# Mixing the first gate pair's products with the spatial gate's in a one-layer decoder kernel

## The chip, the cores and the metric

The kernel runs on one core of one Trainium2 chip. The metric is device time in microseconds (us), the median of three runs. Five engines work from queues of their own, each in the order in which its instructions were written: TensorE (PE in the profile, its weight loads PEld), VectorE (DVE), ScalarE (ACT), GpSimd (POOL) and SyncE (SP), which here only issues transfers (DMA).

## The reference

One layer over a sequence of 1024 positions and 1024 features, all in float32:

```
h = rmsnorm(x)
[q | k | v | u | s | gate_a | gate_b] = h @ w_in
A = sliding-window attention(q, k, v)            (window 128, 8 heads, ALiBi, sinks)
B = gelu(u) * (tril(W_s) @ rmsnorm(gelu(s)) + b) (per channel group, in chunks of 128 positions)
x = x + (sigmoid(gate_a) * (A @ w_oa) + sigmoid(gate_b) * (B @ w_ob)) @ w_out
x = x + down( silu(conv_g) * conv_v ),  conv = causal depthwise width-3 conv of up(rmsnorm(x))
```

The change lies between B, the spatial gate, and the projections gate_a and gate_b.

## The kernel before

Every matrix product is made in three TensorE passes: each float32 operand is split into a high part (rounded to the type that TensorE multiplies at full rate) and a low part (what is left), and high·high, high·low and low·high are added. A split is an ACT copy that makes the high part (`copy_hi`, L76) and a subtraction on DVE or POOL that makes the low part.

The gate projections, 16 output tiles of 128 features by 1024 positions, are computed in eight pairs: a pair takes one tile of gate_b and the same tile of gate_a. Each pair is a two-by-two block product by Winograd's form of Strassen's scheme: seven products instead of eight. A product (`Blocks.prod`, L916) is 12 matmuls of 128x512: four blocks of the inner dimension, three passes each. The left operands are weights: A11 and A12 are the tile of gate_b, A22 is half of the tile of gate_a, and S1 to S4 are sums of them, made on POOL. The right operands are B11, B21, B22 (parts of the input, split long before) and T1 to T4 (sums of parts of the input, made in place in the tiles `xa`). The seven products are A11·B11, A12·B21, S4·B22, A22·T4, S1·T1, S2·T2 and S3·T3. `split_p` makes the high and low parts of A11 and A12, `split_q` those of S1 and A22, `split_r` those of S2 and S4 (tile `gax`), `split_s3` those of S3; their low parts come from POOL (L885). `x_split` (L747) makes those of T1 to T4 in two halves of 128x1024 each, with both low parts on DVE (L756).

The spatial gate works in four channel tiles t and two halves of the sequence, so eight products (t, half). `sgu_seed` (L812, an ACT copy) fills a PSUM tile with the bias b, `sgu_mm` (L818) adds 12 matmuls of 128x256 onto it, and `sgu_mul` (L827, two DVE instructions) multiplies the result into `uT`. A seed can be written when the PSUM tile that it takes has been read by the `sgu_mul` that used it last. The right factors are the v rows: eight row blocks s, each passed through gelu (`v_gelu`), normed (`v_norm`) and split (`v_split`) into `vsh` and `vsl`.

The order is written out by hand, and nothing reorders it. `v_phase` (L767) computes the v rows, with the products (0,0), (1,0) and (2,0) between them, and other preparation hung on its steps by the table `X_WORK` (the first half of T1 at step 5). Then come (3,0) and (0,1) to (3,1) one after another (L1709 to L1714), the second half of T1 and both of T3, and then `gates` (L1104): `first_gate_pair` (L993) and seven times `gate_pair` (L1028). In `first_gate_pair` T2 and T4 are split on DVE while the products run. A pair prepares the weights of the next (`nx`). T1, T2 and T4 each take a tile of the pool whose tiles carry the tag Y, and T4 can be written only when one of the raw tiles `xa` has been read for the last time. PSUM holds four tiles of 128x1024: two in pool psA and, once the v rows are through, two in pool psC.

Of the kernel before, what the change touches and what calls it, by code (L numbers as in the profile page):

```python
# [10 lines left out]
F = mybir.dt.float32  # L11
# [30 lines left out]
def body(ctx, tc, nc, a):  # L42
# [33 lines left out]
    def copy_hi(dst, src, scale=1.0):  # L76
        return nc.scalar.activation(dst, src, AF.Copy, scale=scale)  # L77

    def mm3(out, wh, wl, mh, ml, first, last, **kw):

        nc.tensor.matmul(out, wh, mh, start=first, stop=False, **kw)  # L81
        nc.tensor.matmul(out, wh, ml, start=False, stop=False, **kw)  # L82
        nc.tensor.matmul(out, wl, mh, start=False, stop=last, **kw)  # L83
# [655 lines left out]

    def v_norm(s):  # L740
        nc.vector.scalar_tensor_tensor(vg_[s], vg_[s], vss_[s][:, 0:1], sg_b, op0=ALU.mult, op1=ALU.mult)

    def v_split(s):
        copy_hi(vsh[:, s, :], vg_[s])
        nc.vector.tensor_tensor(vsl[:, s, :], vg_[s], vsh[:, s, :].bitcast(F), op=ALU.subtract)

    def x_split(n, ks=range(2)):  # L747
        r, c = {"T1": (0, L), "T3": (0, H), "T2": (1, H), "T4": (1, L)}[n]
        if n not in xb:
            xb[n] = zr[0].tile([128, 2, 4, 512], R, tag="Z", name="T3") if n == "T3" else \  # L750
                Y(n, R, [128, 2, 4, 512])
        for k in ks:
            kk = slice(2 * k, 2 * k + 2)
            src = xr_raw[r][:, kk, c]
            copy_hi(xb[n][:, 0, kk, :], src)
            nc.vector.tensor_tensor(xb[n][:, 1, kk, :], src, xb[n][:, 0, kk, :].bitcast(F), op=ALU.subtract)  # L756
# [55 lines left out]
    def sgu_seed(t, half):  # L812

        pm = pms[t, half] = PS("pm")
        nc.scalar.activation(pm.rearrange("p (n i) -> p n i", i=128),
                             bs_b[:, t:t + 1, :].to_broadcast([128, 8, 128]), AF.Copy)
# [23 lines left out]
    class Left:  # L840
# [152 lines left out]
    def first_gate_pair():  # L993

        w, nx = g_left[0], g_left[1]
        q = Blocks(w.w, xb)
        e = PS("pe")
        psum["P"].insert(0, psum["P"].pop())
        m5, m7 = e[:, L], e[:, H]
# [14 lines left out]
        nx.split_p()
        q.prod(m7, "S3", "T3")
        nc.scalar.copy(x7, m5)
        nc.vector.tensor_tensor(q.g1, x7, q.g1, op=ALU.add)
        nc.vector.tensor_tensor(x7, x7, m7, op=ALU.add)
# [682 lines left out]
    jobs.append((None, 0, None))  # L1701
    with tc.manual_schedule():
        v_phase()
        psB.__exit__(None, None, None)
        psum["C"] = tc.tile_pool(name="psC", bufs=2, space=bass.MemoryType.PSUM, reuse_waits="tile")
        psC = psum["C"].__enter__()
        psum["P"] = [psC, psC, psA, psA]
        psum["H"] = None
        order = [(3, 0)] + [(t, 1) for t in range(4)]  # L1709
        for i, m in enumerate(order):  # L1710
            if i < 4:
                sgu_seed(*order[i + 1])
            sgu_mm(*m)
            sgu_mul(*m)  # L1714
        x_split("T1", (1,))
        x_split("T3")
        sg_cm.__exit__(None, None, None)
        gates_open()
        psum["P"] = [psC, psC, psA, psA]
        g_left[1].load_p()  # L1720
# [70 lines left out]
```

## Time and profile before

| what | value |
|---|---|
| median of 3 runs | 1215.3 us (1214.7 to 1215.97) |
| the profiled execution, its own time | 1215.15 us |
| its span, first to last instruction | 1213.4 us |
| granted TensorE clock, mean over the span | 0.994 |
| TensorE busy | 1188.4 us, 98% of the span |
| DVE, POOL, ACT busy | 894.8, 568.6, 542.4 us |

A row of the timeline gives the start in us from the span's beginning, the duration in us, the engine, the line of the kernel, the operation, the output and the inputs by tile name, and the shapes; `xN` says that N equal instructions stand merged, and brackets hold the idle time of the engine ahead of the instruction and what ended it. `pm` is a PSUM tile of the spatial gate, `pz` and `pe` are PSUM tiles of the gate pairs, `T` is a tile of T1 to T4 (and of other right operands), `x` of the L920 rows is the input's split tiles, `ph`, `pl`, `qh`, `ql`, `s3h`, `s3l` are weight parts, `lp`, `lq`, `lr` raw weights. A row of waits gives who waited, for whom, the us in total, how often, and the longest. A row of windows gives for a stretch the busy us and the instructions of each engine, the granted clock (1.00 is full), the share of DMA and its rate.

### The profile page before, as it was taken

To read this page: it belongs to the slowest core of one execution; us is meant where nothing else is said; L and a number is where in the kernel's file an instruction comes from. 1 tells how busy PE (TensorE), PEld (TensorE's weight loads), DVE (VectorE), ACT (ScalarE), POOL (GpSimd) and SP (SyncE) were. 2 spreads that over 40 slices of the span, in tenths; PEclk is the share of its full clock that TensorE was granted. 3 is DMA by queue.
4 is the path that set the end of the run, shared out by engine and by line. 5 is a ranking of instruction groups with operands and counts; after the bars stand their busy time and mean duration, and the time that the engine had idled before them with its cause. 6 is when DMAs were issued, how large, how long until landed. Compare 5 with 4: busy or idle time off the path is not lost.

```text
span 1213.4 us, 15834 instructions
## 1 busy us (share of the span) xinstructions
PE 1188.4 (98%) x5866; PEld 1005.1 (83%) x5866; DVE 894.8 (74%) x1033; ACT 542.4 (45%) x830; POOL 568.6 (47%) x360
## 2 busy tenths in 40 slices
PE   9999999889999999999999999999999999999998
PEld 8889989868887888888788888888888888888886
DVE  7688966764465665568787888877888888776674
ACT  8455575733444312223544444444544445524331
POOL 2467583277766522334765756657565642000000
PEclk9999999989999999999999999999999999999999
DMA  7010143125777897442223324233342358975472
GB/s 280 21 53 19 53 140 122 54 77 173 251 256 270 295 343 274 159 161 104 88 97 112 137 102 144 95 114 125 110 147 87 122 173 276 383 252 191 143 227 73
DMA packets 78989, 191.27 MB, mean 158 GB/s; under 512 B 8896, under 2 KB 9152, under 8 KB 78912
## 3 DMA queue, kind: packets, MB, share of 16 engines
q1 hardware_dynamic: 78912, 190.26, 45.0%
q8 instruction: 46, 0.75, 0.3%
q14 instruction: 31, 0.25, 0.1%
HBM read 139.63 MB, written 50.59 MB: 157 GB/s over the span
## 4 chain that ended last, share of the span: by engine, by line
PE 84%; DVE 7%; ACT 2%; DMA 1%; issue 1%; POOL 0%; SPq 0%; DVEq 0%; ACTq 0%
PE pz L920 42%; PE pd L1601 10%; PE pdy L1601 7%; PE px L81 2%; PE po L82 2%; PE po L81 2%; PE px L83 2%; PE px L82 2%; PE po L83 2%; DMA ls<-wup 1%; PE pvs L81 1%; DVE T L756 1%; PE pvs L83 1%; PE pvs L82 1%; PE pq L81 1%
## 5 line engine op out<-in xcount | busy, mean ns | idle before, releaser
L920 PE MATMUL pz<-T,qh 128*128 128x512 f32 x464 | 142.8, 389 | 0.0
L885 POOL TENSOR_TENSOR pl<-lp,ph 128x1024 fp32r<-128x1024 f32 x30 | 73.6, 2452 | 83.6 <-ACT ph L77 83.5
L920 PE MATMUL pz<-B,ph 128*128 128x512 f32 x352 | 109.5, 392 | 0.0
L920 PEld LDWEIGHTS pz<-T,qh 128*128 128x128 f32 x464 | 87.1, 188 | 18.0
L920 PE MATMUL pz<-T,ql 128*128 128x512 f32 x232 | 90.2, 389 | 0.0
L98 POOL TENSOR_TENSOR wjl<-wj,wjh 128x512 fp32r<-128x512 f32 (+1 forms) x24 | 40.6, 1692 | 95.7 <-ACT wjh L77 95.7
L885 POOL TENSOR_TENSOR ql<-lq,qh 128x1024 fp32r<-128x1024 f32 x30 | 77.6, 2587 | 14.5 <-ACT qh L77 14.5
L920 PEld LDWEIGHTS pz<-B,ph 128*128 128x128 f32 x352 | 65.3, 188 | 15.4 <-ACT x L1449 1.9
L935 DVE TENSOR_TENSOR pz<-pz,rstd_b 128x1024 f32<-128x1024 f32 x60 | 73.9, 1232 | 4.6 <-ACT rstd_b L131 2.5
L885 POOL TENSOR_TENSOR s3l<-s,s3h 128x512 fp32r<-128x512 f32 x30 | 41.2, 1373 | 71.9 <-ACT s3h L77 64.0
L920 PE MATMUL pz<-T,s3h 128*128 128x512 f32 x232 | 71.4, 389 | 0.0
L920 PE MATMUL pz<-B,pl 128*128 128x512 f32 x176 | 68.5, 389 | 0.0
L1601 PE MATMUL pd<-bh,ah 128*128 128x512 f32 x176 | 68.5, 389 | 0.0
L1601 PE MATMUL pd<-bl,ah 128*128 128x512 f32 x176 | 68.5, 389 | 0.0
L1601 PE MATMUL pd<-bh,al 128*128 128x512 f32 x176 | 68.5, 389 | 0.0
L920 PE MATMUL pz<-T,AX 128*128 128x512 f32 x264 | 64.9, 396 | 0.0
L920 PE MATMUL pz<-B,AX 128*128 128x512 f32 x264 | 63.4, 389 | 0.0
L77 ACT ACTIVATE qh<-lq 128x1024 fp32r<-128x1024 f32 x30 | 31.9, 1062 | 64.8 <-issue 35.1
L920 PEld LDWEIGHTS pz<-T,AX 128*128 128x128 f32 x264 | 50.6, 192 | 10.6
L920 PEld LDWEIGHTS pz<-B,AX 128*128 128x128 f32 x264 | 49.5, 188 | 10.3
L1307 DVE SCALAR_TENSOR_TENSOR tv<-pz,cp,tv 128x1023 f32<-128x1023 f32 (+1 forms) x44 | 56.2, 1278 | 0.8
L1307 DVE SCALAR_TENSOR_TENSOR tg<-pz,cp,tg 128x1023 f32<-128x1023 f32 (+1 forms) x44 | 56.2, 1278 | 0.8
(334 smaller groups left out, 3563.7 us busy)
## 6 DMA issues: line engine op xcount, KB each, us to landing
ls<-wup SPq DMA_DIRECT2D x22, 512.0 KB, 5.4
sum<-ls SPq DMA_DIRECT2D x22, 512.0 KB, 4.9
lp<-wup SPq DMA_DIRECT2D x22, 512.0 KB, 3.5
ra<-wdown SPq DMA_DIRECT2D x44, 256.0 KB, 4.7
b<-T SPq DMA_DIRECT2D x44, 256.0 KB, 3.7
B<-tv SPq DMA_DIRECT2D x33, 256.0 KB, 2.0
T<-tt SPq DMA_DIRECT2D x33, 256.0 KB, 2.1
b<-B SPq DMA_DIRECT2D x33, 256.0 KB, 3.2
```

Source lines behind the costliest of these rows:

```text
L77: return nc.scalar.activation(dst, src, AF.Copy, scale=scale)
L81: nc.tensor.matmul(out, wh, mh, start=first, stop=False, **kw)
L82: nc.tensor.matmul(out, wh, ml, start=False, stop=False, **kw)
L83: nc.tensor.matmul(out, wl, mh, start=False, stop=last, **kw)
L98: nc.gpsimd.tensor_tensor(l[:, :nk, :], r[:, :nk, :], h[:, :nk, :].bitcast(F), op=ALU.subtract)
L756: nc.vector.tensor_tensor(xb[n][:, 1, kk, :], src, xb[n][:, 0, kk, :].bitcast(F), op=ALU.subtract)
L885: nc.gpsimd.tensor_tensor(l, r, h.bitcast(F), op=ALU.subtract)
L920: nc.tensor.matmul(o, p[:, k, :], y[:, q, k, :], start=not more and k == 0 and j == 0, stop=k == 3 and j == 2, skip_group_check=True)
L935: nc.vector.tensor_tensor(z, z, rstd_b, op=ALU.mult)
L1307: nc.vector.scalar_tensor_tensor(t[:, j:], p[:, 0:1024 - j], cw[:, ci, 2 - j:3 - j], t[:, j:], op0=ALU.mult, op1=ALU.add)
L1601: nc.tensor.matmul(o[d], p[:, k - k0, m], q[:, k - k0, :], start=new and k == 0 and j == 0, stop=k == HK - 1 and j == 2, skip_group_check= ...
```

## The change

Four things are altered, all ahead of the second gate pair.

- **The v rows' tiles.** `vsh` and `vsl` (8 row blocks each) become two sets of 4 blocks, `vs[0]` and `vs[1]`. The first set lies with the two tiles `vg` in a pool of its own, `sa`, which closes after product (3,0); the gate pairs' temporaries (`gp`, with `gax`) are then opened at the other end of the memory. `ls`, the pool that the weight sums of the later MLP load into, opens only when the second set is through (`sums_open`). The row sums `vss` become columns of one tile.
- **T2 split among the v rows.** Step 5 of `v_phase` now splits the first half of T2 (where the first half of T1 was), and step 6, which had no such work, the second half, on ACT and DVE ahead of `sgu_mul(0, 0)`.
- **The order.** The products (3,0) and (0,1) to (3,1) move into `first_gate_pair`. TensorE's order becomes (3,0), A11·B11, A12·B21, (0,1), S2·T2, (1,1), S3·T3, (2,1), (3,1), S4·B22, S1·T1, A22·T4. The pair's two PSUM tiles are in psC from the start, and the seeds alternate in the two tiles of psA. S2·T2 is now added onto A11·B11 in PSUM; A22·T4 is added onto S3·T3 there as before, and S1·T1 gets a PSUM tile of its own (`e`).
- **Where the low parts are made.** T3's and T4's go from DVE to POOL; those of S1 and A22 of the first pair go from POOL to DVE, in halves (128x512 each); T1 is split as a whole between A12·B21 and `sgu_mul(0, 1)`.

The core of the diff:

```diff
-    vsh = sg.tile([128, 8, 512], R, name="vsh")
-    vsl = sg.tile([128, 8, 512], R, name="vsl")
+    vs = {1: [sg.tile([128, 4, 512], R, name="vs" + x) for x in "hl"]}
+    sa = sa_cm.__enter__()
+    vgt = [sa.tile([128, 512], F, name=f"vg{i}") for i in range(2)]
+    vs[0] = [sa.tile([128, 4, 512], R, name="vs" + x) for x in "hl"]
...
-        5: lambda: x_split("T1", (0,)),
+        5: lambda: x_split("T2", (0,)),
+        6: lambda: x_split("T2", (1,)),
...
+        def split_q(self, halves=False):
+            h, l = (wst.tile([128, 8, 128], R, tag="w" + x, name=nm("q" + x)) for x in "hl")
+            if not halves:
+                self.split(("S1", "A22"), self.q, h, l)
+                return
+            for n, k in (("S1", slice(0, 4)), ("A22", slice(4, 8))):
+                copy_hi(h[:, k], self.q[:, k])
+                nc.vector.tensor_tensor(l[:, k], self.q[:, k], h[:, k].bitcast(F), op=ALU.subtract)
+                self.w[n] = h[:, k], l[:, k]
...
     def gates_open():
+        pools["gp_cm"] = tc.tile_pool(name="gp", bufs=1, side="right")
+        gp = pools["gp"] = pools["wx"] = pools["gp_cm"].__enter__()
+        pools["AX"] = gp.tile([128, 2, 1024], R, name="gax")
+
+    def sums_open():
         pools["ls_cm"] = tc.tile_pool(name="ls", bufs=1)
         pools["ls"] = pools["ls_cm"].__enter__()
...
         sums_load()
...
         w, nx = g_left[0], g_left[1]
+        psB.__exit__(None, None, None)
+        psum["C"] = tc.tile_pool(name="psC", bufs=2, space=bass.MemoryType.PSUM, reuse_waits="tile")
+        psC = psum["C"].__enter__()
+        psum["H"] = None
+        psum["P"] = [psC]
         q = Blocks(w.w, xb)
...
+        psum["P"] = [psA]
+        x_split("T3", eng=nc.gpsimd)
+        sgu_mm(3, 0)
+        sgu_seed(0, 1)
+        sa_cm.__exit__(None, None, None)
+        gates_open()
         x1, x7, q.u2 = q.temps()
         w.split_r()
         q.prod(q.v1, "A11", "B11")
         nc.scalar.copy(x1, q.v1)
-        w.split_q()
+        sgu_mul(3, 0)
+        w.split_s3()
         q.prod(q.g0, "A12", "B21")
+        sgu_seed(1, 1)
+        sgu_mm(0, 1)
+        nc.vector.tensor_tensor(q.g0, x1, q.g0, op=ALU.add)
+        x_split("T1")
+        sgu_mul(0, 1)
+        q.prod(q.v1, "S2", "T2", more=True)
+        nc.scalar.copy(q.u2, q.v1)
+        sgu_seed(2, 1)
+        sgu_mm(1, 1)
+        sgu_mul(1, 1)
+        q.prod(q.v0, "S3", "T3")
+        nc.scalar.copy(x7, q.v0)
+        sgu_seed(3, 1)
+        g_left[1].load_p()
+        sgu_mm(2, 1)
+        sgu_mul(2, 1)
+        x_split("T4", eng=nc.gpsimd)
+        sgu_mm(3, 1)
+        w.split_q(halves=True)
+        sgu_mul(3, 1)
+        sg_cm.__exit__(None, None, None)
+        sums_open()
+        e = PS("pe")
+        psum["P"] = [psA, psA, psC, psC]
         nx.load_q()
...
         q.prod(q.g1, "S4", "B22")
...
+        nx.split_p()
+        q.prod(e[:, L], "S1", "T1")
         nx.sums_q()
...
         nx.split_s3()
+        nc.vector.tensor_tensor(x7, x7, e[:, L], op=ALU.add)
+        nc.vector.tensor_tensor(x1, q.u2, e[:, L], op=ALU.add)
         nx.sums_r()
...
+        q.prod(q.v0, "A22", "T4", more=True)
         nx.split_q()
         g_left[2].load_p()
...
+        nc.vector.tensor_tensor(q.v1, x7, q.v1, op=ALU.add)
+        nc.vector.tensor_tensor(q.v0, q.u2, q.v0, op=ALU.add)
+        q.scale(q.zv)
+        q.u2 = x1
         return q
```

More of the change, by code (lines that the diff above doesn't have):

```diff
@@ L123, in body @@
     ss_b = base.tile([128, 8], F, name="ss_b")
-    base.tile([128, 88], F, name="base_pad")
+    vss8 = base.tile([128, 8], F, name="vss8")
+    base.tile([128, 80], F, name="base_pad")
     def rms_rows(pb, diag, hs=(0, 1)):
@@ L717, in body @@
     sg = sg_cm.__enter__()
+    sa_cm = tc.tile_pool(name="sa", bufs=1)
     rb = sg.tile([128, 1024], F, name="rb")
@@ L726, in body @@
     wgl = wst.tile([128, 8, 128], R, tag="wl", name="wgl")
-    vg_, vss_ = {}, {}
+    vg_ = {}
     xb = {"B11": xq[0][0], "B21": xq[1][0], "B22": xq[1][1]}
@@ L731, in v_gelu, with x_split @@
         p = pvs.pop(s)
-        vg = vg_[s] = sg.tile([128, 512], F, tag="vg", name=nm("vg"), bufs=2)
+        vg = vg_[s] = vgt[s % 2]
         nc.scalar.activation(vg, p, AF.Gelu_apprx_tanh, scale=rstd[:, s:s + 1])
-        ss = vss_[s] = sg.tile([128, 1], F, tag="vss", name=nm("vss"), bufs=2)
-        nc.scalar.activation(p, vg, AF.Square, accum_out=ss)
+        nc.scalar.activation(p, vg, AF.Square, accum_out=vss8[:, s:s + 1])
     def v_rsqrt(s):
-        rsqrt_cols(vss_[s], vss_[s], 1, 512)
+        rsqrt_cols(vss8[:, s:s + 1], vss8[:, s:s + 1], 1, 512)
     def v_norm(s):
-        nc.vector.scalar_tensor_tensor(vg_[s], vg_[s], vss_[s][:, 0:1], sg_b, op0=ALU.mult, op1=ALU.mult)
+        nc.vector.scalar_tensor_tensor(vg_[s], vg_[s], vss8[:, s:s + 1], sg_b, op0=ALU.mult, op1=ALU.mult)
     def v_split(s):
-        copy_hi(vsh[:, s, :], vg_[s])
-        nc.vector.tensor_tensor(vsl[:, s, :], vg_[s], vsh[:, s, :].bitcast(F), op=ALU.subtract)
-    def x_split(n, ks=range(2)):
+        h, l = (t[:, s % 4, :] for t in vs[s // 4])
+        copy_hi(h, vg_[s])
+        nc.vector.tensor_tensor(l, vg_[s], h.bitcast(F), op=ALU.subtract)
+    def x_split(n, ks=range(2), eng=None):
         r, c = {"T1": (0, L), "T3": (0, H), "T2": (1, H), "T4": (1, L)}[n]
@@ L755, in x_split @@
             copy_hi(xb[n][:, 0, kk, :], src)
-            nc.vector.tensor_tensor(xb[n][:, 1, kk, :], src, xb[n][:, 0, kk, :].bitcast(F), op=ALU.subtract)
+            (eng or nc.vector).tensor_tensor(xb[n][:, 1, kk, :], src, xb[n][:, 0, kk, :].bitcast(F),
+                                             op=ALU.subtract)
     X_WORK = {
@@ L820, in sgu_mm @@
         for ci in range(4):
-            s = 4 * half + ci
             c = slice(t * 128, (t + 1) * 128)
             g = slice(2 * t, 2 * t + 2)
-            mm3(pm[:, ci * 256:(ci + 1) * 256], vsh[:, s, c], vsl[:, s, c],
+            mm3(pm[:, ci * 256:(ci + 1) * 256], vs[half][0][:, ci, c], vs[half][1][:, ci, c],
                 wgh[:, g, :], wgl[:, g, :], False, True, skip_group_check=True)
@@ L891, in split_p @@
                                                  for x in "hl"))
-        def split_q(self):
-            self.split(("S1", "A22"), self.q, *(wst.tile([128, 8, 128], R, tag="w" + x, name=nm("q" + x))
-                                                for x in "hl"))
+        def split_q(self, halves=False):
[7 more added lines that the diff above has]
+                self.w[n] = h[:, k], l[:, k]
         def split_s3(self):
@@ L978, in gates_open @@
     def gates_open():
+        pools["gp_cm"] = tc.tile_pool(name="gp", bufs=1, side="right")
+        gp = pools["gp"] = pools["wx"] = pools["gp_cm"].__enter__()
+        pools["AX"] = gp.tile([128, 2, 1024], R, name="gax")
+    def sums_open():
         pools["ls_cm"] = tc.tile_pool(name="ls", bufs=1)
         pools["ls"] = pools["ls_cm"].__enter__()
-        pools["gp_cm"] = tc.tile_pool(name="gp", bufs=1)
-        gp = pools["gp"] = pools["wx"] = pools["gp_cm"].__enter__()
-        pools["AX"] = gp.tile([128, 2, 1024], R, name="gax")
         sums_load()
@@ L1003, in first_gate_pair @@
         nc.scalar.copy(x1, q.v1)
-        w.split_q()
+        sgu_mul(3, 0)
+        w.split_s3()
         q.prod(q.g0, "A12", "B21")
+        sgu_seed(1, 1)
[22 more added lines that the diff above has]
+        psum["P"] = [psA, psA, psC, psC]
         nx.load_q()
-        w.split_s3()
-        x_split("T2")
         q.prod(q.g1, "S4", "B22")
-        q.prod(m5, "S1", "T1")
-        nc.vector.tensor_tensor(q.g0, x1, q.g0, op=ALU.add)
-        x_split("T4")
+        nx.split_p()
+        q.prod(e[:, L], "S1", "T1")
         nx.sums_q()
[L1014 to L1018, printed above, removed]
         nx.split_s3()
+        nc.vector.tensor_tensor(x7, x7, e[:, L], op=ALU.add)
+        nc.vector.tensor_tensor(x1, q.u2, e[:, L], op=ALU.add)
         nx.sums_r()
-        q.prod(q.v1, "S2", "T2")
+        q.prod(q.v0, "A22", "T4", more=True)
         nx.split_q()
         g_left[2].load_p()
-        q.prod(m7, "A22", "T4", more=True)
-        q.sums(x1, x7, m7)
+        nc.vector.tensor_tensor(q.v1, x7, q.v1, op=ALU.add)
+        nc.vector.tensor_tensor(q.v0, q.u2, q.v0, op=ALU.add)
+        q.scale(q.zv)
+        q.u2 = x1
         return q
@@ L1703, in body @@
         v_phase()
[L1704 to L1720, printed above, removed]
         gates()
```

3 lines of the change are left out of this document (removed).

## The prediction

> **What bounds the kernel now.** I read the page first, then TensorE's waits, then the stretch in which they fall by windows and row by row.
>
> ```profile
> span 1213.4 us, 15834 instructions
> PE 1188.4 (98%) x5866; PEld 1005.1 (83%) x5866; DVE 894.8 (74%) x1033; ACT 542.4 (45%) x830; POOL 568.6 (47%) x360
> ```
> ```profile
> PE pe L920 <- DVE x L1018: 5.5, 1, 5.5
> PE pm L81 <- ACT pm L815: 3.2, 2, 2.1
> ```
> ```profile
> 222.60:231.00 8.40, 5.22 (x29) 4.83 (x28) 5.74 (x10) 5.78 (x9) 0.55 (x1) 0.80 0.01 3
> 250.00:262.80 12.80, 7.32 (x26) 5.59 (x25) 8.74 (x7) 1.14 (x3) 9.26 (x5) 0.73 0.14 42
> ```
>
> TensorE is busy for 98% of the span, so only its idle time can be won. Its largest waits, 8.7 us of the 25 idle, lie in two stretches that the change rewrites: the seeds of the spatial gate (222.6 to 231) and the first gate pair's last product (250 to 262.8). In both the granted clock is also down, to 0.80 and 0.73. TensorE's own rows show how:
>
> ```profile
> 222.50 0.28 PE L83 MATMUL pm<-wgh,vsl 128*128 128x256 f32 x1
> 223.85 0.38 PE L81 MATMUL pm<-wgh,vsh 128*128 128x256 f32 x1 [1.07 <-ACT pm L815]
> ...
> 227.66 0.58 PE L81 MATMUL pm<-wgh,vsh 128*128 128x256 f32 x1 [2.11 <-ACT pm L815]
> ...
> 231.00 0.27 PE L81 MATMUL pm<-wgh,vsh 128*128 128x256 f32 x1
> ...
> 236.38 0.63 PE L920 MATMUL pz<-x,ph 128*128 128x512 f32 x2
> ...
> 244.57 0.61 PE L920 MATMUL pe<-T,qh 128*128 128x512 f32 x2
> ...
> 247.29 0.61 PE L920 MATMUL pe<-T,s3h 128*128 128x512 f32 x2
> ...
> 250.01 2.92 PE L920 MATMUL pz<-T,gax 128*128 128x512 f32 x12
> 258.41 1.19 PE L920 MATMUL pe<-T,qh 128*128 128x512 f32 x2 [5.49 <-DVE x L1018]
> ...
> 262.76 0.63 PE L920 MATMUL pz<-x,ph 128*128 128x512 f32 x2
> ...
> 265.50 0.62 PE L920 MATMUL pz<-T,s3h 128*128 128x512 f32 x2
> ...
> 270.94 0.62 PE L920 MATMUL pz<-T,qh 128*128 128x512 f32 x2
> ```
>
> Two prices come from here. A product of a pair takes 2.72 us (244.57 to 247.29). The 45 spatial matmuls from 231.00 to 236.38 take 0.12 each, so 12 take 1.44. The 15 before them, from 227.66 to 231.00, take 0.223 each at about half the clock: 1.55 us lost. A22·T4, from 258.41 to 262.76, takes 4.35 instead of 2.72: 1.63 lost. Ahead of it 5.68 are lost (8.40 from the start of S2·T2, which takes 2.72). Why A22·T4 waits, DVE shows, with ACT behind:
>
> ```profile
> 217.25 1.23 DVE L756 TENSOR_TENSOR T<-xa,T 128x1024 fp32r<-128x1024 f32 x1 [0.26 <-ACT T L77]
> ...
> 220.84 1.39 DVE L832 TENSOR_TENSOR uT<-pm,uT 64x512 f32<-64x512 f32 x2
> ...
> 225.09 1.39 DVE L832 TENSOR_TENSOR uT<-pm,uT 64x512 f32<-64x512 f32 x2
> ...
> 228.91 1.39 DVE L832 TENSOR_TENSOR uT<-pm,uT 64x512 f32<-64x512 f32 x2
> ...
> 238.07 13.27 DVE L756 TENSOR_TENSOR T<-xa,T 128x1024 fp32r<-128x1024 f32 x5
> ...
> 251.98 4.89 DVE L756 TENSOR_TENSOR T<-xa,T 128x1024 fp32r<-128x1024 f32 x2
> ...
> 257.58 0.69 DVE L1018 TENSOR_TENSOR x<-x,pe 128x512 f32<-128x512 f32 x1
> ```
> ```profile
> 219.46 0.62 ACT L77 ACTIVATE vsh<-vg 128x512 fp32r<-128x512 f32 x1
> ...
> 222.79 1.01 ACT L815 ACTIVATE pm<-rb 128x1024 f32<-128x1024 f32 x1
> ...
> 226.58 1.03 ACT L815 ACTIVATE pm<-rb 128x1024 f32<-128x1024 f32 x1 [2.22 <-DVE uT L832]
> ...
> 246.90 2.02 ACT L77 ACTIVATE T<-xa 128x1024 fp32r<-128x1024 f32 x2 [3.61 <-DVE T L756]
> ...
> 250.21 0.59 ACT L1016 COPY x<-pe 128x512 f32<-128x512 f32 x1 [0.35 <-PE pe L920]
> ```
>
> Seven low parts of T stand in DVE's queue from 238.07 to 256.87. Each takes 2.4 to 2.65 us there, against 1.23 at 217.25 when POOL was idle. The sum at L1018, which must read `pe` before A22·T4 may add to it, is queued behind them. POOL is slowed at the same time:
>
> ```profile
> 237.81 2.40 POOL L885 TENSOR_TENSOR gax<-lr,gax 128x1024 fp32r<-128x1024 f32 x1 [14.04 <-ACT gax L77]
> 240.96 2.60 POOL L885 TENSOR_TENSOR ql<-lq,qh 128x1024 fp32r<-128x1024 f32 x1 [0.75 <-ACT qh L77]
> ...
> 245.86 2.16 POOL L611 TENSOR_TENSOR s<-lp,lq 128x512 f32<-128x512 f32 x1
> ...
> 250.22 3.37 POOL L885 TENSOR_TENSOR pl<-lp,ph 128x1024 fp32r<-128x1024 f32 x1
> 253.55 2.24 POOL L885 TENSOR_TENSOR s3l<-s,s3h 128x512 fp32r<-128x512 f32 x1
> ...
> 258.07 1.27 POOL L611 TENSOR_TENSOR lr<-lp,lr 128x512 f32<-128x512 f32 x1
> ...
> 274.10 2.40 POOL L885 TENSOR_TENSOR pl<-lp,ph 128x1024 fp32r<-128x1024 f32 x1
> 276.45 1.30 POOL L885 TENSOR_TENSOR s3l<-s,s3h 128x512 fp32r<-128x512 f32 x1
> ```
>
> Alone POOL takes 2.40 for 128x1024 and 1.30 for 128x512; beside DVE up to 3.37 and 2.24.
>
> **The change, step by step.** TensorE does the same matmuls, so I follow the new order until S1·T1 of the second pair, which began at 270.94.
>
> *T2 among the v rows.* Its first half replaces T1's at step 5, at no cost. The second half, at step 6, is new on both queues. ACT makes its high part behind the row at 219.46, until 221.0, in a gap. DVE then needs 1.23, and `sgu_mul(0, 0)`, queued behind it, moves from 220.84 to 222.2. It ends at 223.6, and the seed of (2,0), which takes that PSUM tile, moves from 222.79 to 223.7. What follows is one chain: seed, copy of a v row, its low part, `sgu_mul(1, 0)` (225.09 to 226.0), seed of (3,0) (226.58 to 227.5), product (3,0) (227.66 to 228.55). **Cost 0.9 us**; the wait ahead of (2,0) grows from 1.07 to 2. Bounds: 0, if DVE fits it into gaps, to 1.55, the full move of `sgu_mul(0, 0)` with its wait.
>
> *The half clock there.* TensorE again stands still twice for about 2 us. I take the clock to come back at 231.0 as before. Then 11 matmuls of (3,0) run slowly, 1.1 us lost instead of 1.55: **gain 0.45**. Bounds: nothing lost (1.55 gained), or slow for another 3.3 us (1.6 more lost). [...]
>
> *From (3,0) to (3,1).* (3,0) ends at 231.05. A11·B11 and A12·B21 need nothing late; (0,1) starts at 236.5 and S2·T2 at 237.9. S2's low part: the high parts of T3 pass ACT from 229.0 to 230.9. POOL makes T3's low parts until 234.8 and `gax` until 237.2, 0.7 ahead of S2·T2. That cover is thin: beside DVE (3.37 each) it would be 3 late, but DVE's work until 237.4 reads PSUM with one SBUF operand, and the one kind of overlap that slowed both above had two. (1,1) starts at 240.65, S3·T3 at 242.1, (2,1) at 244.8.
>
> The seeds now alternate in two PSUM tiles. T1's low parts follow A12·B21 on DVE (237.4 to 239.8), then `sgu_mul(0, 1)` until 241.2, the seed of (2,1) until 242.4: 2.4 early. With T1 at 2.65 each it is 0.5 late, the bound. The seed of (3,1) stands on ACT behind the copy of S3·T3 (0.59, like the row at 250.21): 245.0 plus 0.59 plus 1.03 gives 246.6, where TensorE is free at 246.25. **Cost 0.3.** (3,1) ends at 248.0, S4·B22 at 250.7.
>
> *T4, S1 and A22.* T4's high parts follow on ACT from 246.45 to 248.5 (T1 and T3 have read `xa` by 239.8, so the wait of 3.61 is gone). POOL makes the low parts from 247.5 to 252.3. S1's and A22's high parts (0.62 each) end on ACT at 249.7, and DVE makes their low parts, 0.69 each alone, by 250.5. S1·T1 starts at 250.7 and ends at 253.4, A22·T4 at 253.4 instead of 258.41, and the second pair at 256.2 instead of 262.76. **The stall of 5.68 and its half clock of 1.63 are gone: 7.3 us.** L1018's successor reads a tile of its own, so nothing waits for it.
>
> *What is late next: POOL.* Behind T4 it has the second pair's weights: `pl` until 254.7, two sums 257.3, `s3l` 258.6, two sums 261.2, `ql` 263.6. Needed: `pl` at 256.2, `s3l` 258.9, `ql` 264.3. The two low parts on DVE meet T4 on POOL. I charge POOL half of their 1.4 us, 0.7: `s3l` is there at 259.3, `ql` at 264.3. **Cost 0.4, at the second pair's S3·T3.** Bounds: 0, and the first rival. Their raw weights (`lq`) are requested after `ls`, which waits for (3,1):
>
> ```profile
> lq<-wga SPq DMA_DIRECT2D x8, 512.0 KB, 3.9
> ```
>
> Requested at about 249, past `ls`'s two requests on SP's queue, they land near 253 and are first read at 254.7. With `ls` taking the same engines they may be 2 late at worst, in the first rival's direction. In later pairs POOL has 13.7 us of work (three of 2.40 at 128x1024, five of 1.30) for 19 of TensorE, and is ahead again.
>
> *Sum.* 5.68 + 1.63 + 0.45 − 0.9 − 0.3 − 0.4 = 6.2 us: S1·T1 of the second pair at 264.75 instead of 270.94. After that the kernel is as before, 6.2 earlier, and TensorE-bound. Against the profiled execution's 1215.15 that is 1208.95; the median shown is 0.15 above it, inside its runs' spread. **Forecast 1209.1 us.**
>
> **Rivals.** *POOL becomes the bound.* All its work from 247.5 takes the crowded prices: T4's low parts 3.37 each until 254.2 (A22·T4 0.8 late), `pl` 257.6, sums of 2.16 until 261.9, `s3l` 264.2, sums 267.7, `ql` 270.3. S1·T1 starts at 270.4, and 0.5 is left: **1214.6**. For it speak the rows at 250.22 and 253.55; against it, that seven DVE instructions with two SBUF inputs crowded POOL there, and now two of half the size do.
>
> *DVE is shut out.* The low part of S1 is ready on DVE at 249.1, while POOL holds T4's. If POOL, with its queue full, kept DVE out until its first gap, at about 261.3, S1·T1 would start at 262.1, lose 1.6 to the half clock, and the second pair would begin at 271.9, 9.1 later than before: **1224**, slower. It makes the kernel measurably slower from a wait of about 8.6 us on, the gain of 6.2 and 0.2%. Against it: in the 13.27 us with five DVE low parts, POOL worked almost throughout and DVE still finished one every 2.65. [...]
>
> *It does not do what it says: T4 is as late as before.* From 246.90 to 256.87 T4 took 10 us. If it took 10 from 246.45, A22·T4 would start at 256.4 instead of 253.4. POOL's `pl`, sums and `s3l` would then follow until 262.7, 0.8 behind TensorE, and S1·T1 start at 268.1: **1212.4**. Against it, DVE's queue ahead of T4, which made it 10, is gone.
>
> **How the numbers follow.** The forecast with its own bounds has 0.66: with no half clock, no crowding and T2's cost at half it is about 2 lower (1207.1), with a longer half clock and more crowding 2.4 higher (1211.5). T4 late has 0.09, POOL the bound 0.12, DVE shut out 0.05; 0.03 lie below 1207 and 0.05 elsewhere, as a wait in the new memory places. The range 1207.0 to 1213.6 holds the forecast, T4 late and the milder part of POOL's. About 0.2% (2.4 us) is what a measurement tells from no change: below 1212.9 are the forecast, T4 late, the 0.03 and a little of POOL's, 0.80 in all; 0.14 lie within, 0.06 above 1217.7.
>
> **What would show it.** TensorE's wait for DVE at A22·T4 gone and its matmuls at full clock; waits of about 2 us ahead of (2,0) and (3,0), the latter at 228.5; a short wait for POOL in the second pair's S3·T3. Wrong it would be with a wait for `gax` at S2·T2, low parts on DVE far over 1.4 us, or POOL instructions of over 3 us from 247 on.

## The result, and the profile after

The changed kernel takes **1207.59 us** (median of 4 runs, 1207.17 to 1209.46); the kernel before, run beside it, 1215.05. The ratio is 0.994, with a 95% interval of 0.9923 to 0.9958. The forecast was 1209.1, the range 1207.0 to 1213.6. The profiled execution took 1207.24, its span 1205.5.

From the page of the changed kernel, span and busy time:

```profile
span 1205.5 us, 15823 instructions
PE 1185.8 (98%) x5866; PEld 1002.3 (83%) x5866; DVE 890.2 (74%) x1030; ACT 542.4 (45%) x831; POOL 573.0 (48%) x363
```

TensorE runs the same 5866 matmuls; its busy time fell by 2.6 us and its idle time, span less busy, from 25.0 to 19.7. The waits and the two stretches that the prediction looked at, first the waits of TensorE in the changed kernel, then its windows (start and end, length, busy us of PE, PEld, DVE, ACT and POOL with their instructions, clock, DMA share, GB/s):

```profile
PE pm L81 <- ACT pm L821: 4.2, 3, 2.1
```

```profile
222.60:231.00 8.40, 4.46 (x30) 4.03 (x31) 6.50 (x12) 5.05 (x7) 1.79 (x2) 1.00 0.01 2
250.00:256.50 6.50, 6.50 (x31) 5.37 (x30) 5.98 (x7) 0.63 (x1) 6.42 (x4) 1.00 0.33 120
```

The wait of 5.5 us at A22·T4 is no longer among the waits. The seeds' wait grew from 3.2 to 4.2. The clock is full in both stretches (1.00; at half clock, as the text calls it below, the views give 0.50, as from 228.0 to 230.0 in the kernel before). TensorE's rows show the new order:

```profile
220.94 0.28 PE L81 MATMUL pm<-wgh,vsh 128*128 128x256 f32 x1
...
222.26 0.28 PE L83 MATMUL pm<-wgh,vsl 128*128 128x256 f32 x1
...
224.44 0.38 PE L81 MATMUL pm<-wgh,vsh 128*128 128x256 f32 x1 [1.90 <-ACT pm L821]
...
228.24 0.39 PE L81 MATMUL pm<-wgh,vsh 128*128 128x256 f32 x1 [2.10 <-ACT pm L821]
...
229.78 0.63 PE L931 MATMUL pz<-x,ph 128*128 128x512 f32 x2
...
236.68 2.92 PE L931 MATMUL pz<-T,gax 128*128 128x512 f32 x12
...
245.38 0.39 PE L81 MATMUL pm<-wgh,vsh 128*128 128x256 f32 x1 [0.18 <-ACT pm L821]
...
249.66 0.62 PE L931 MATMUL pe<-T,qh 128*128 128x512 f32 x2
...
252.38 0.62 PE L931 MATMUL pz<-T,qh 128*128 128x512 f32 x2
...
255.09 0.62 PE L931 MATMUL pz<-x,ph 128*128 128x512 f32 x2
...
257.81 0.61 PE L931 MATMUL pz<-T,s3h 128*128 128x512 f32 x2
258.35 0.50 PE L931 MATMUL pz<-T,s3l 128*128 128x512 f32 x1
...
263.48 0.62 PE L931 MATMUL pz<-T,qh 128*128 128x512 f32 x2
```

The row at 220.94 is the first matmul of (1,0); the same one in the kernel before:

```profile
221.18 0.28 PE L81 MATMUL pm<-wgh,vsh 128*128 128x256 f32 x1
```

S1·T1 of the first pair starts at 249.66, A22·T4 right behind it at 252.38, 2.72 later, the second pair at 255.09 (262.76 before), and its S1·T1 at 263.48 (270.94 before). I use the stretch **from (1,0) to S1·T1 of the second pair** as the ruler for all that follows: 221.18 to 270.94 is 49.76 us before, 220.94 to 263.48 is 42.54 after. So 7.22 of the 7.91 between the two profiled executions (1215.15 and 1207.24) lie in it; 0.24 is an earlier start, and the other 0.45 comes behind it.

DVE and POOL in the changed kernel, in the timeline of each:

```profile
220.69 1.23 DVE L760 TENSOR_TENSOR T<-xa,T 128x1024 fp32r<-128x1024 f32 x1 [0.25 <-ACT T L77]
221.93 1.39 DVE L837 TENSOR_TENSOR uT<-pm,uT 64x512 f32<-64x512 f32 x2
...
224.97 0.69 DVE L749 TENSOR_TENSOR vsl<-vg,vsh 128x512 fp32r<-128x512 f32 x1 [0.80 <-ACT vsh L77]
...
247.80 1.55 DVE L905 TENSOR_TENSOR ql<-lq,qh 128x512 fp32r<-128x512 f32 x1 [1.10 <-ACT qh L77]
249.27 2.88 DVE L905 TENSOR_TENSOR ql<-lq,qh 128x512 fp32r<-128x512 f32 x1
```

```profile
232.11 2.43 POOL L760 TENSOR_TENSOR T<-xa,T 128x1024 fp32r<-128x1024 f32 x1
234.47 2.42 POOL L890 TENSOR_TENSOR gax<-lr,gax 128x1024 fp32r<-128x1024 f32 x1
...
246.38 2.43 POOL L760 TENSOR_TENSOR T<-xa,T 128x1024 fp32r<-128x1024 f32 x1 [7.25 <-ACT T L77]
248.75 2.85 POOL L760 TENSOR_TENSOR T<-xa,T 128x1024 fp32r<-128x1024 f32 x1
251.56 2.85 POOL L890 TENSOR_TENSOR pl<-lp,ph 128x1024 fp32r<-128x1024 f32 x1
...
257.00 1.30 POOL L890 TENSOR_TENSOR s3l<-s,s3h 128x512 fp32r<-128x512 f32 x1
```

The two low parts on DVE took 1.55 and 2.88 instead of 0.69 each (the price of a low part of that size with POOL idle, row at 224.97). Each of them ended about half a microsecond behind a row of POOL. DVE's first began at 247.80, 1.0 us before POOL's half of T4 ended at 248.81, and ended 0.5 us later at 249.35. POOL's second half took 0.42 longer than its first, and DVE's second low part ended only at 252.15, half a microsecond behind POOL's row that ended at 251.60. A22·T4 began at 252.38: only 0.23 us of the cover was left. It is no accident of one execution: the two took 4.35 us again in the profiles of the two kernels below that start from this one, "products earlier" and "products earlier, T1 on POOL".

### The profile page after: what moved, and what is told of

It is laid out like the page before. It is cut to its first block, busy times and chain, and to the rows that moved or that the text cites. A ratio compares the mean times of both kernels' runs of the same rounds, so it can differ in the third digit from the quotient of the medians.

```text
span 1205.5 us, 15823 instructions
## 1 busy us (share of the span) xinstructions
PE 1185.8 (98%) x5866; PEld 1002.3 (83%) x5866; DVE 890.2 (74%) x1030; ACT 542.4 (45%) x831; POOL 573.0 (48%) x363
## 4 chain that ended last, share of the span: by engine, by line
PE 84%; DVE 6%; ACT 2%; DMA 2%; issue 1%; POOL 0%; SPq 0%; ACTq 0%; DVEq 0%
PE pz L931 43%; PE pd L1643 10%; PE pdy L1643 7%; PE px L82 2%; PE px L81 2%; PE po L82 2%; PE po L81 2%; PE po L83 2%; PE px L83 2%; DMA ls<-wup 1%; DVE xa L612 1%; PE pv L505 1%; PE pq L81 1%; PE pq L83 1%; PE pq L82 1%
## 5 line engine op out<-in xcount | busy, mean ns | idle before, releaser
L931 PE MATMUL pz<-T,qh 128*128 128x512 f32 x472 | 145.3, 389 | 0.0
L890 POOL TENSOR_TENSOR ql<-lq,qh 128x1024 fp32r<-128x1024 f32 x29 | 75.0, 2587 | 9.1 <-ACT qh L77 9.1
L931 PE MATMUL pz<-T,s3h 128*128 128x512 f32 x240 | 73.9, 389 | 0.0
L612 DVE TENSOR_TENSOR ls<-ls 128x512 f32<-128x512 f32 x44 | 48.7, 1107 | 12.0 <-DMA ls<-wup 11.2
```

The costliest lines, as they stand in the source:

```text
L612: eng.tensor_tensor(out, x, y, op=op)
L890: nc.gpsimd.tensor_tensor(l, r, h.bitcast(F), op=ALU.subtract)
L931: nc.tensor.matmul(o, p[:, k, :], y[:, q, k, :], start=not more and k == 0 and j == 0, stop=k == 3 and j == 2, skip_group_check=True)
```

## The experiments

The theory was that the low parts of T2, T3 and T4 held up L1018 on DVE, that handing them to other engines takes that stall away, and that the mixed order is what gives them the time. The rivals: the new engine assignment alone does it; POOL becomes the bound; the half clock, not the stall, decides. Each kernel was timed beside the kernel before on the same chip.

| kernel | median us | runs | lowest, highest | ratio to before, 95% | ruler, us |
|---|---|---|---|---|---|
| before | 1215.05 | 4 | 1214.7, 1215.97 | | 49.76 |
| changed | 1207.59 | 4 | 1207.17, 1209.46 | 0.994, 0.9923 to 0.9958 | 42.54 |
| changed, again | 1208.09 | 6 | 1206.03, 1209.61 | 0.9945, 0.993 to 0.996 | 44.10 |
| changed, a third time | 1207.19 | 6 | 1205.72, 1210.88 | 0.9941, 0.9928 to 0.9955 | 42.57 |
| engines alone, old order | 1213.13 | 11 | 1209.67, 1217.57 | 0.9984, 0.9971 to 0.9998 | 48.97 |
| engines balanced, old order | 1212.14 | 12 | 1210.36, 1216.62 | 0.9979, 0.9965 to 0.9994 | 48.66 |
| T3 and T4 on DVE | 1209.54 | 5 | 1207.38, 1211.05 | 0.9954, 0.9942 to 0.9967 | 44.32 |
| T2 later | 1207.74 | 5 | 1206.47, 1208.18 | 0.9938, 0.9924 to 0.9952 | 43.21 |
| waits filled | 1207.22 | 5 | 1205.24, 1208.9 | 0.9935, 0.9922 to 0.9947 | 42.56 |
| S1, A22 on POOL | 1213.36 | 12 | 1210.6, 1216.01 | 0.9989, 0.9978 to 1.0001 | 47.44 |
| products earlier | 1206.03 | 6 | 1204.95, 1210.59 | 0.9936, 0.9917 to 0.9955 | 41.02 |
| products earlier, T1 on POOL | 1203.25 | 5 | 1202.84, 1206.84 | 0.9911, 0.9898 to 0.9925 | 39.23 |

The ruler is that of the profiled execution alone, and says which stage a difference comes from; the medians are over all runs, and a difference of under 1 us between them is not resolved. The changed kernel stood again beside "engines balanced", "S1, A22 on POOL" and "products earlier" (the second time) and beside the last kernel of the table (the third), not beside the other four.

### Engines alone, in the old order of TensorE

Edit, to the kernel before: T2 is split at steps 5 and 6 of the v rows, T1 whole on DVE and T3 on POOL behind the spatial gate, T4 on POOL. TensorE's order is that of before. It is not the whole assignment of the change: the low parts of S1 and A22 stay on POOL.

```diff
-        5: lambda: x_split("T1", (0,)),
+        5: lambda: x_split("T2", (0,)),
+        6: lambda: x_split("T2", (1,)),
...
-        x_split("T2")
         q.prod(q.g1, "S4", "B22")
...
-        x_split("T4")
+        x_split("T4", eng=nc.gpsimd)
...
-        x_split("T1", (1,))
-        x_split("T3")
+        x_split("T1")
+        x_split("T3", eng=nc.gpsimd)
```

> The kernel before, with only the places of the splits changed: T2 among the v rows (steps 5 and 6), T1 as a whole and T3 behind the spatial gate, low parts of T3 and T4 on POOL. TensorE's order stays as before: all products of the spatial gate, then the pair's. Theory: the stall at A22*T4 goes with DVE's queue alone, but POOL now stands ahead of S4*B22 with T3's two low parts (4.8 us and more beside DVE) before gax, which costs 2 to 3 us there; S1*T1 of the second pair about 4.4 us earlier than before: 1210.7 (1209.7 to 1211.7), with TensorE waiting for gax at S4*B22. Rival, the mixing of the products is what carries the gain: 1214 or more, with A22*T4 still waiting several us.

Measured: 1213.13, a ratio of 0.9984. Its TensorE and POOL rows, in their timelines:

```profile
245.39 4.63 PE L922 MATMUL pz<-x,gax 128*128 128x512 f32 x10 [3.85 <-POOL gax L887]
```

```profile
236.30 5.75 POOL L756 TENSOR_TENSOR T<-xa,T 128x1024 fp32r<-128x1024 f32 x2 [11.54 <-ACT T L77]
242.01 3.33 POOL L887 TENSOR_TENSOR gax<-lr,gax 128x1024 fp32r<-128x1024 f32 x1
```

The median lies between the theory's 1209.7 to 1211.7 and the rival's 1214. The trace has the theory's mechanism and not the rival's: the wait at A22·T4 is gone, and TensorE waits in an earlier product, S4·B22, for `gax`. But the wait is 3.85 us where the theory had 2 to 3, and the half clock, which it left out, comes behind it: ten matmuls take 4.63 (granted clock 0.72 from 240 to 252). T3's low parts hold POOL from 236.30 to 242.05, and `gax`, queued behind them, ends at 245.34. In the old order only two products, 235.46 to 240.93, lie ahead of S4·B22 to cover these 9 us.

### Engines balanced, in the old order

Edit, to the kernel above: T3's low parts go back to DVE, so that POOL is free for `gax`.

```diff
-        x_split("T3", eng=nc.gpsimd)
+        x_split("T3")
```

> As e1_splits_alone (TensorE's order of the kernel before), but with T3's low parts on DVE, so that POOL has gax, the low parts of S1, A22 and S3, and T4's. Theory, with e1's result: without the mixing either POOL or DVE has more to do than the products cover; with the load balanced the wait for gax at S4*B22 goes and 2 to 3 us are left, at S1*T1 and for the second pair's weights behind T4 on POOL: 1210.8 (1209.8 to 1212). Rival, the mixing wasn't needed, only the balance: 1208.5 or less. Other rival, without the mixing nothing is won: 1213 or more.

Measured: 1212.14, just above the theory's band (to 1212), 2.4 below the kernel before beside it (1214.56). Its TensorE row, and POOL's behind it:

```profile
261.35 0.79 PE L922 MATMUL pz<-x,pl 128*128 128x512 f32 x1 [2.33 <-POOL pl L887]
```

```profile
251.60 4.76 POOL L756 TENSOR_TENSOR T<-xa,T 128x1024 fp32r<-128x1024 f32 x2 [3.39 <-ACT T L77]
```

The stall has moved once more, to the second pair's `pl`, which stands on POOL behind T4 and two sums, as the theory expected; T4 itself began late, at 251.60. At A22·T4 0.2 us of wait are left. This is the best that I found for the old order: two ways of sharing out the same low parts won 2.1 and 2.4 us, against 6.5 to 7.5 with the new order. In both, **the old order lacked the time for the splits**. That no assignment would do in the old order is not shown: neither run moves S1 and A22 to DVE, as the change does.

### S1 and A22 back on POOL, in the new order

Edit, to the changed kernel: the first pair's S1 and A22 are split as a whole, with the low parts on POOL.

```diff
-        w.split_q(halves=True)
+        w.split_q()
```

> The changed kernel with the low parts of S1 and A22 of the first pair made as a whole on POOL again. Theory: they stand behind T4's low parts, until about 253.5 where S1*T1 needs them at 249.7: TensorE waits 3.9 us there, loses up to 1.6 to the half clock after it, and A22*T4 follows: 1211.5 to 1213. Rival, POOL has room (DVE was the bound): within 1 us of the changed kernel.

Measured: 1213.36, just above the theory's 1211.5 to 1213, and no longer told apart from the kernel before (the interval reaches 1.0001). Its TensorE and POOL rows:

```profile
253.30 0.50 PE L931 MATMUL pe<-T,ql 128*128 128x512 f32 x1 [3.21 <-POOL ql L890]
```

```profile
250.91 2.34 POOL L890 TENSOR_TENSOR ql<-lq,qh 128x1024 fp32r<-128x1024 f32 x1
```

`ql` waits on POOL behind T4's low parts, S1·T1 stands still for 3.21 us (3.9 expected), and the half clock follows, from 253.9 to 257.3. The ruler is 4.9 us longer than in the changed kernel, and the median 5.3 above that of the changed kernel beside it (1208.09). So this small part of the change, two instructions moved to DVE, decides over more than half of the gain, even though they run there at three times their own price (4.35 us for the two, 0.69 each alone). The run leaves T4 on POOL ahead of them; with T4 on DVE as well, which would be the new order with the old engines throughout, no run was made.

### T3 and T4 on DVE, in the new order

Edit, to the changed kernel: `eng=nc.gpsimd` is left out for both.

```diff
-        x_split("T3", eng=nc.gpsimd)
+        x_split("T3")
...
-        x_split("T4", eng=nc.gpsimd)
+        x_split("T4")
```

> The changed kernel with the low parts of T3 and T4 back on DVE (the other parts kept). Theory: DVE has room for four of 1.23 us in the new order (3.2 us idle ahead of 235.5, 2.4 ahead of 245.3), POOL is relieved, and nothing of it lies on TensorE's path but about 0.2 us at S1*T1: 1207.6, within 0.5 of the changed kernel. Rival, POOL's share carries the gain: the low parts take 2.4 to 2.65 us on DVE as in the kernel before, S1*T1 and A22*T4 start 2 or more late: 1209.5 or more.

Measured: 1209.54. The median is the rival's, but the trace does not bear out the rival's reason. Its rows on DVE, the window of the seeds' waits, and TensorE's first matmul of (0,1), in this run and in the changed kernel:

```profile
231.83 2.36 DVE L760 TENSOR_TENSOR T<-xa,T 128x1024 fp32r<-128x1024 f32 x2
...
249.31 2.36 DVE L760 TENSOR_TENSOR T<-xa,T 128x1024 fp32r<-128x1024 f32 x2
```

```profile
221.00:231.00 10.00, 6.37 (x38) 5.88 (x37) 7.88 (x12) 6.50 (x10) 0.55 (x1) 0.75 0.01 2
```

```profile
237.83 0.28 PE L81 MATMUL pm<-wgh,vsh 128*128 128x256 f32 x1
```

```profile
235.24 0.28 PE L81 MATMUL pm<-wgh,vsh 128*128 128x256 f32 x1
```

Each low part takes 1.18 us on DVE with POOL idle. The clock, 0.75 in the window of the seeds, was down from 226.0 to 232.9, into A11·B11. From (0,1) to S1·T1 of the second pair (265.84), where the clock is full in both, this execution takes 28.01 us and the changed one 28.24: leaving T3 and T4 on DVE costs nothing there, and no wait at A22·T4 comes back. Its ruler is longer by 1.8 us, all of it ahead of (0,1), where the clock was down. The runs reach from 1207.38 to 1211.05, and whether the assignment as such costs anything over many executions stays open.

### T2's second half later

Edit, to the changed kernel: step 6 is left out, and the second half of T2 is split behind `sgu_mul(3, 0)`.

```diff
-        6: lambda: x_split("T2", (1,)),
...
         sgu_mul(3, 0)
+        x_split("T2", (1,))
```

> The changed kernel with the second half of T2 split behind sgu_mul(3, 0) instead of at step 6. Theory (the chain through sgu_mul(0, 0) and the seed of (2,0)): product (2,0) starts 0.9 earlier, the wait ahead of it falls from 1.90 to about 1.1, and all that follows moves with it: 0.9 less than the changed kernel, about 1206.7; T2's low part is ready about 1 us ahead of S2*T2. Rival, the wait is set by something else, or is given back at S2*T2: 1207.6 as the changed kernel.

Measured: 1207.74. Its TensorE rows at (2,0) and (3,0), and the window:

```profile
222.95 0.39 PE L81 MATMUL pm<-wgh,vsh 128*128 128x256 f32 x1 [1.01 <-ACT pm L820]
...
226.75 0.39 PE L81 MATMUL pm<-wgh,vsh 128*128 128x256 f32 x1 [2.11 <-ACT pm L820]
```

```profile
221.00:231.00 10.00, 6.88 (x38) 5.99 (x38) 7.41 (x12) 7.38 (x11) 3.27 (x3) 0.85 0.01 2
```

The wait ahead of (2,0) falls from 1.90 to 1.01, and (3,0) starts 6.41 after (1,0) (220.34) instead of 7.30: the 0.89 that the prediction charged for T2. In this execution the half clock, with 0.85 in the window, took it back, and the medians do not tell the two kernels apart. The cost of T2's place is shown in the trace and not in the time.

### The waits filled with matmuls

Edit, to the changed kernel: 7 and 8 matmuls of 128x512 into a PSUM tile of their own, in the waits ahead of (2,0) and (3,0).

```diff
+    def fill(p, n):
+        for _ in range(n):
+            nc.tensor.matmul(p, wgh[:, 0, :], hx(0, 0, L), start=True, stop=True)
...
+        p_fill = PH("fill")
+        fill(p_fill, 7)
         sgu_mul(1, 0)
...
+        fill(p_fill, 8)
         sgu_mul(2, 0)
```

> The changed kernel with 7 and 8 more matmuls of 128x512 into an unused PSUM tile in the two waits ahead of (2,0) and (3,0); their results are not used. Theory: the two waits of about 2 us bring the half clock in some executions and not in others (the kernel before lost 1.55 us there in its profiled execution, the changed one nothing in its own). With TensorE kept busy no execution loses it: the median falls by 0 to 0.7 us and the runs lie closer together; 1207.0. Rival, the runs' differences come from elsewhere: the same median and spread as the changed kernel, or up to 0.5 more where a filling matmul delays a product.

Measured: 1207.22, 0.4 us below the changed kernel and within the spread of both. TensorE's waits in its profile:

```profile
PE pm L81 <- ACT pm L829: 0.7, 3, 0.3
```

The waits are filled, and the clock is 1.00 in the window of the seeds; but it is 1.00 there in two of three executions of the changed kernel too. That filling keeps the clock up is neither shown nor excluded: the runs (1205.24 to 1208.9) are not clearly closer together than those of the changed kernel.

### The changed kernel twice more

No edit; both stood beside other experiments on the same chip.

> The changed kernel itself, once more on the chip of these runs, to be compared with the others: 1207.5, runs from 1206.5 to 1209.5 with the half clock in some and not in others.

> The changed kernel itself, beside e9_t1_on_pool on the same chip: 1207.8, 3 to 4 us above it by the theory, 1.5 by the rival.

Measured: 1208.09 and 1207.19, with a wider spread than expected (1205.72 to 1210.88 over both). Two windows of the first of these profiles, then the same two of the second:

```profile
221.00:231.00 10.00, 5.96 (x46) 5.56 (x45) 7.88 (x12) 6.49 (x10) 0.83 (x2) 0.97 0.01 2
231.00:250.00 19.00, 18.82 (x100) 16.23 (x100) 9.49 (x13) 11.81 (x15) 9.19 (x5) 0.92 0.00 0
```

```profile
221.00:231.00 10.00, 5.98 (x48) 5.58 (x47) 7.66 (x12) 6.49 (x10) 1.02 (x2) 1.00 0.00 0
231.00:250.00 19.00, 18.82 (x107) 16.37 (x106) 12.16 (x14) 13.27 (x18) 11.49 (x5) 1.00 0.02 6
```

It is the same program, and the seeds' waits are the same 4.2 us in all three (longest 2.1): in one execution the clock falls (0.97 and 0.92), in the other two it stays up. The ruler is 44.10 with the fall and 42.54 and 42.57 without, **1.53 to 1.56 us apart**; the prediction read 1.55 from the profile before as the price of one slow stretch. The fall does not explain the whole spread, though: the second of these two profiles has no fall and is yet of the slowest execution of its six (1210.88), 3.6 us above the first profile of the changed kernel (1207.24). Its (1,0) starts 1.5 us later, and the rest comes behind the ruler.

### Products earlier

If the seeds' waits are the next loss, a product put into them should win it. Edit, to the changed kernel: A11·B11 runs between (1,0) and (2,0), A12·B21 behind (3,0), T2's second half goes behind `sgu_mul(2, 0)`, T3's low parts to DVE, and `gax` is first on POOL.

```diff
+        q = pair_open()
+        q.prod(q.v1, "A11", "B11")
         sgu_mul(1, 0)
...
+        x_split("T2", (1,))
         sgu_mm(3, 0)
...
         w.split_r()
-        q.prod(q.v1, "A11", "B11")
+        sgu_seed(0, 1)
         nc.scalar.copy(x1, q.v1)
+        q.prod(q.g0, "A12", "B21")
         sgu_mul(3, 0)
+        x_split("T3")
         w.split_s3()
-        q.prod(q.g0, "A12", "B21")
         sgu_seed(1, 1)
         sgu_mm(0, 1)
+        sgu_mul(0, 1)
         nc.vector.tensor_tensor(q.g0, x1, q.g0, op=ALU.add)
         x_split("T1")
-        sgu_mul(0, 1)
```

> The changed kernel with A11*B11 placed between (1,0) and (2,0), where TensorE waits for a seed, the second half of T2 behind sgu_mul(2, 0), gax first on POOL and T3's low parts on DVE. Theory: A11*B11 needs nothing that is late, so it fills the wait ahead of (2,0); the chain to (3,0) is 0.9 shorter without T2; what is left are about 0.8 us ahead of (3,0) and 0.4 ahead of (3,1), and with waits that short no half clock: S1*T1 of the second pair 3 to 3.7 us earlier than in the changed kernel: 1204.0. Rival, the chain of seeds and sums through ACT and DVE paces the stretch, not TensorE's order: the waits come back at (0,1) or S2*T2 and the time stays above 1206.5.

Measured: 1206.03, between the theory's number and the rival's. Its rows at (3,1) on TensorE, and DVE's ahead of it:

```profile
244.70 0.38 PE L81 MATMUL pm<-wgh,vsh 128*128 128x256 f32 x1 [2.00 <-ACT pm L823]
```

```profile
233.55 4.13 DVE L760 TENSOR_TENSOR T<-xa,T 128x1024 fp32r<-128x1024 f32 x2
...
239.87 2.36 DVE L760 TENSOR_TENSOR T<-xa,T 128x1024 fp32r<-128x1024 f32 x2
242.15 2.81 DVE L839 TENSOR_TENSOR uT<-pm,uT 64x512 f32<-64x512 f32 x4
```

The waits ahead of (2,0) and (3,0) are 0 and 0.28 now, but a new one of 2.00 stands at (3,1): its seed waits for `sgu_mul(1, 1)`, which is among the four instructions behind T1's low parts on DVE. T3's took 4.13 instead of 2.36, beside `gax` and `s3l` on POOL.

### Products earlier, T1 on POOL

POOL stood idle for 9.1 us there, from `s3l` to T4. Edit, to the kernel above: one argument.

```diff
-        x_split("T1")
+        x_split("T1", eng=nc.gpsimd)
```

> e5_products_earlier with T1's low parts on POOL, which stood idle from 236.6 to 245.7 there. Theory, from its trace: the wait of 2.00 ahead of (3,1) comes from sgu_mul(1, 1) behind T3's and T1's low parts on DVE; without T1's it ends near 241.3 and (3,1) waits 0.3 instead of 2.0. S1*T1 of the second pair 1.7 earlier, 1204.2. POOL's T4 and the second pair's weights move along, so its wait at the second pair's S3*T3 stays at about 0.3. Rival, POOL becomes late with S1*T1 or the second pair: no better than e5_products_earlier, 1206.

Measured: **1203.25**, 0.9911 of the kernel before and 3.9 below the changed kernel beside it (1207.19). TensorE at (3,1) and at S1·T1 of the second pair:

```profile
242.73 0.39 PE L81 MATMUL pm<-wgh,vsh 128*128 128x256 f32 x1 [0.18 <-ACT pm L823]
...
260.83 0.62 PE L933 MATMUL pz<-T,qh 128*128 128x512 f32 x2
```

The wait of 2.00 is 0.18. The ruler, 221.60 to 260.83, is 39.23, 3.3 below the 42.57 of the changed kernel beside it. The move alone shortens the ruler by 1.8 us (41.02 before it), forecast 1.7; the median is 1 us below the theory's 1204.2. It is the fastest version found.

## Why the prediction was right, and where it was off

The forecast was of the right sign and size: 1209.1 against 1207.59, and 1207.99 over all 16 runs of the changed kernel. By its terms, in the profiled execution (gains +, costs −):

| term | forecast, us | measured, us |
|---|---|---|
| the wait at A22·T4 | +5.68 | +5.68 (no wait left) |
| its half clock | +1.63 | +1.63 (2.71 from 252.38 to 255.09) |
| the half clock at (3,0) | +0.45 | +1.55 (none) |
| T2's second half in the v rows' chain | −0.9 | −0.82 |
| the seed of (3,1) | −0.3 | −0.4 |
| `s3l` late for the second pair's S3·T3 | −0.4 | −0.2 |
| sum | 6.2 | 7.4; the ruler gives 7.2 |

**The stall at A22·T4** went as the prediction said, and so did its half clock. The experiments qualify the reason. It was not enough that the low parts left DVE: with the old order the stall was found again at `gax` (3.85) and at `pl` (2.33), and in the new order with S1 and A22 on POOL at `ql` (3.21). On the other side it was not needed that T3's and T4's low parts left DVE: in the new order, with both on DVE, no wait at A22·T4 came back. So the new order is what kept the stall from turning up elsewhere, and with T4 on POOL it needed S1 and A22 on DVE; whether it would have done with the old engines throughout is open.

The new order also takes DVE out of the dependence that ended the wait before. There the sum L1018, on DVE, had to read `pe` first. Now A22·T4 is added onto S3·T3 in `pz`, which a copy on ACT reads 8 us earlier:

```profile
243.81 0.59 ACT L1039 COPY x<-pz 128x512 f32<-128x512 f32 x1 [1.17 <-PE pz L931]
```

The prediction has this in half a sentence ("L1018's successor reads a tile of its own"). Before, T4's own low parts ended at 256.87 and L1018 at 258.27, so by these rows the dependence was worth an estimated 1.4 of the 5.5 us.

**T2.** (3,0) starts 7.30 after (1,0) (220.94 to 228.24), before 6.48 (221.18 to 227.66): 0.82, predicted 0.9. DVE's two rows at 220.69 and 221.93 are the place, `sgu_mul(0, 0)` moved from 220.84 to 221.93. With T2 elsewhere the 0.89 came back.

**The half clock at (3,0)** is the term that was mis-sized, by 1.1 us. The prediction took the clock to stay down until 231.0 as before; in the profiled execution it did not go down at all, in another of the same kernel it did, from 230.5 to 233.9. It is no property of the order alone, and a single profile, that of before, could not tell that. The bounds (nothing lost, or slow for longer) held it. That the sum comes so near is in part luck: by the ruler the gain is 5.7 us in the profile with the fall and 7.2 in the two without, and the forecast of 6.2 lies between them.

**The seed of (3,1).** From S2·T2 at 236.68 to (3,1) at 245.38 are 8.70 us, for two products of 2.72 and two of 1.44, 8.32: 0.4 late, forecast 0.3. **`s3l`:** from S3·T3 at 257.81 to S1·T1 at 263.48 are 5.67 us for two products, 5.44 before (265.50 to 270.94): 0.2 lost, forecast 0.4. `pl` ended at 254.41, ahead of 255.09.

**POOL as the bound** did not happen. T4's low parts took 2.43 and 2.85, `pl` 2.85, and `s3l` took POOL's own price again (1.30 at 257.00); the rival charged 3.37 for each of the large ones and 2.16 and more for the small ones. `lq` landed in time: POOL's first sum with it follows `pl` without a wait.

**DVE shut out** did not happen either, but the prediction's charge for it was far too small: two low parts of 1.4 us were to end at 250.5; they took 4.35 us, from 247.80 to 252.15. The step that failed is "DVE makes their low parts, 0.69 each alone". The prediction named low parts far over 1.4 us as a sign of being wrong, and the sign came; that it cost nothing was luck: S1's low part ended 0.31 us ahead of S1·T1, A22's 0.23 ahead of A22·T4. In DVE's and POOL's rows together the ends alternate: T4's first half ends at 248.81, DVE's first low part 0.54 later, T4's second half at 251.60, DVE's second 0.55 later, `pl` at 254.41. DVE was not kept out until a gap of POOL, as the rival had it. (The 2.4 to 2.65 that the prediction read for each of DVE's crowded low parts are means over merged rows; singly they took 2.3 to 3.4.)

**`gax`** was to be ready 0.7 ahead of S2·T2; its row ends at 236.89, 0.2 after S2·T2's first matmul at 236.68. It cost nothing that the rows show, but that cover is used up: POOL made T3's low parts and `gax` at its own price (2.43, 2.42), and TensorE was 1.2 earlier than forecast.

**T4 as late as before** did not happen: POOL worked on it from 246.38 to 251.60, where the prediction had 247.5 to 252.3.

## What to carry to other kernels

Handing an engine's work to another moved a stall here to the next thing in that engine's queue: three assignments, two in the old order and one in the new, left a stall of 2.3 to 3.9 us at another matmul. It was gone where the order of the engine that waits was changed as well, so that something ready lies in between, and the queues fitted that order. Where VectorE and GpSimd both make sums of two SBUF operands, do not plan with the time that each takes alone (here 0.69 us became 1.55 and 2.88 on VectorE, 2.43 became 2.85 on GpSimd), and look for the place where one of them is idle instead. After a reorder, read the waits again from the start: two later moves, found from the changed kernel's own waits, won another 4 us.

## What the runs showed of the hardware that was not expected

**The half clock came in some executions and not in others, for about 3.4 us or twice that.** Around two waits of 1 to 2.2 us, with a product of 1.4 us between, TensorE went to half clock in some executions and not in others, of one and the same program too. By the granted clock in windows of 1 us it was down from 227.5 to 230.9 in the profile before and from 230.5 to 233.9 in one profile of the changed kernel (there 1.3 us after the second wait had ended), and not at all in its two others. Each of these two slow stretches lasted about 3.4 us and cost 1.53 to 1.56 us of the ruler. In "engines balanced" (227.2 to 234.1) and "T3 and T4 on DVE" (226.0 to 232.9) it was down twice as long, 6.8 us; the first and the last window of the latter:

```profile
226.00:227.00 1.00, 1.00 (x7) 1.00 (x7) 0.99 (x2) 0.00 (x0) 0.00 (x0) 0.51 0.00 0
...
232.00:233.00 1.00, 1.00 (x4) 0.79 (x4) 1.00 (x2) 1.00 (x2) 0.00 (x0) 0.57 0.00 0
```

None of the waits at these drops was over 2.23 us. Behind the longer ones, of 2.33, 3.21, 3.85 and 5.49 us, the clock was down each time.

**VectorE and GpSimd slowed each other.** A low part of 128x512 that took DVE 0.69 us alone took 1.55 and 2.88 beside POOL, one of 128x1024 went from 1.18 to 2.07 on average (half of 4.13), and POOL's went from 2.43 to 2.85. In these rows the loss fell mostly on the engine with the shorter instructions: in the changed kernel DVE's two took 4.35 us, 3.0 more than alone (twice 0.69), and POOL's two beside them, T4's second half and `pl`, 0.42 and 0.45 more (2.85 each, for 2.43 and 2.40).
